# A hybrid attention, HGRN2 and mixture-of-experts block: two-operand work moved from GpSimd to VectorE, token-major mixer outputs, and an affine step moved behind a gather

## The chip, the core and the metric

The kernel runs on one core of one Trainium2 chip. The metric is device time in microseconds, the median of three runs. One execution was also taken by the hardware profiler; all rows below are from it. Engines: TensorE (PE, with its weight loads PEld), VectorE (DVE), ScalarE (ACT), GpSimd (POOL) and SyncE (SP), which issues most transfers.

## What is computed

One encoder block on 256 tokens of width 1024, with 16 learned meta tokens in front (272 rows, all float32):

```
h    = layer_norm(concat(meta, x), ln_emb)
qa, ka, va, qb, fb, ib, gb = split(h @ w_in)              # 1024 x 3584
ya   = diff_attention(qa, ka, va)    # 4 heads, rope, chunk-causal, a = p0 - lam * p1, rms_norm per head
yb   = hgrn2(qb, fb, ib, gb)         # 4 heads, gated linear recurrence, rms_norm per head, * silu(g)
h    = layer_norm(alpha * h + concat(ya, yb) @ w_out, ln1)
ffn  = moe(h)                        # 32 experts, top 4 of each token, clamped SwiGLU
h    = layer_norm(alpha * h + ffn, ln2);  return h without the meta tokens
```

## The kernel before

The program has a first part (to about 204 us) that does everything up to the router, and a second part, the experts.

*Pieces.* w_in comes in 28 pieces of 128 output features (512 KB each), w_out in 8. `split(i)` takes a raw piece and makes two parts of it whose sum is the float32 weight: hi, a cast on ScalarE (L178), and lo = raw - hi (L180). The engine of the lo part is GpSimd for i < 3 and for odd i, 20 of 36 pieces, and VectorE for the rest. There are three slots for hi and lo each and four for raw pieces. `project i` runs 24 matmuls, for each of 8 blocks of k the products hi*hH, hi*hL and lo*hH, where hH and hL are the hi and lo parts of the normalised tokens, which VectorE makes block by block at the start (L241, L242). Its result goes on through a `post`, a function by kind of piece.

*The order.* TensorE's instructions stand in the order of the table STEPS, one line for a piece and what follows it; the other engines' order is made by the scheduler. The steps: `diagonal` and `level 0` to `level 7` are the HGRN2 recurrence as a doubling scheme (products of decays, L414, L416 and L418, the matmuls L408), `rope_q`, `rope_k` the rotations, `scores`, `turn` and `values_a` the attention, `out_a` and `out_b` the heads' outputs (features by tokens), `norm r` (the function `fin`) their rms norm with a column sum on TensorE (L496), a root on ScalarE (L498) and a reciprocal of 128x256 on VectorE (L499), `mix a n` the product with a piece of w_out. `residual` multiplies h by the first layer norm's gain and adds its bias on GpSimd (L291, L292), `fold` prepares the router. `begin`, `prefetch` and `close` release space or start the loads of expert weights.

*Behind the last mix.* total1, turn1, logits, choose and position make the second layer norm, the router's choice and each token's place in its expert. `affine(a)` normalises h and applies gain and bias (for half of the tokens' columns on VectorE, L676 and L677, the rest on ScalarE and GpSimd, L678 to L680). `gather` picks the tokens of the experts by a matmul with a 0/1 matrix G (L715) and copies the result to XT (L719).

*Experts.* Experts are served in units of 1 to 4 by the number of their tokens, each with six chunks of 2 MB that are streamed into ten buffers. L779 is the gate and up product, L793 the down product, `begin_acc` (L897, L898) starts the sum over experts with alpha * h and the down biases.

## Time and profile before

| | us |
|---|---|
| runs | 1130.12, 1131.45, 1132.07; median 1131.45 |
| profiled execution | 1132.66 (span 1130.8) |
| TensorE busy | 1007.2 (89%) |
| VectorE busy | 337.3 (30%) |
| ScalarE busy | 177.2 (16%) |
| GpSimd busy | 99.2 (9%) |
| moved by DMA | 428.44 MB, mean 379 GB/s |
| first matmul of the first expert (L779) | at 204.43 |

A busy share is an average over parts with different limits. In the page's forty slices the DMA engines are busy for 3 to 8 tenths up to the eighth slice and for 9 or more from the ninth (from 226 us on) to the thirty-ninth; GpSimd works in the first seven slices alone, apart from the last. A timeline row is: start, duration, engine, line, operation, out<-in and shape, how often, and in brackets how long the engine had been idle and which instruction ended that. A granted clock (PEclk) of 1.00 is 2.4 GHz, 0.50 is 1.2 GHz.

### The profile page before, as it was taken

What the parts mean: (1) busy time and instruction counts of PE and PEld (TensorE: products, weight loads), DVE (VectorE), ACT (ScalarE), POOL (GpSimd) and SP (SyncE); (2) the same over time, 40 slices, a digit from 0 to 9 for tenths busy, and PEclk for the clock granted to TensorE, in tenths of its full rate; (3) what the DMA queues carried; (4) which work ended last, traced back from release to release, by engine and by line L of the source; (5) the groups of instructions that cost most, each with busy time, mean ns of one, the idle gap of its engine ahead of it and who ended that gap; (6) DMA issues with size and microseconds to landing.
All of it is one profiled execution on the core that took longest, in us unless ns stands there. A gap on an engine that the chain in (4) does not pass through costs nothing.

```text
span 1130.8 us, 14815 instructions
## 1 busy us (share of the span) xinstructions
PE 1007.2 (89%) x6066; PEld 525.7 (46%) x6067; DVE 337.3 (30%) x721; ACT 177.2 (16%) x394; POOL 99.2 (9%) x91
## 2 busy tenths in 40 slices
...
GB/s 216 268 216 109 160 223 304 340 416 400 426 428 427 427 429 427 427 427 427 428 427 426 428 429 427 427 428 428 428 426 427 428 428 429 424 429 427 428 409 129
DMA packets 37022, 428.44 MB, mean 379 GB/s; under 512 B 4388, under 2 KB 4772, under 8 KB 12758
## 3 DMA queue, kind: packets, MB, share of 16 engines
...
q10 hardware_dynamic: 628, 0.74, 0.2%
...
## 4 chain that ended last, share of the span: by engine, by line
PE 71%; DMA 14%; DVE 6%; ACT 1%; issue 1%; POOL 0%; DVEq 0%; ACTq 0%; POOLq 0%
PE ps_pj L779 21%; DMA wchunk<-in_wexp 14%; PE ps_pj L793 10%; PE ps_s L715 5%; PE ps_pj L864 5%; PE ps_pj L319 4%; PE ps_s L828 4%; PE ps_pj L836 4%; PE ps_pj L828 4%; PE ps_s L897 3%; PE ps_pj L876 2%; PE ps_g L752 1%; PE ps_pj L774 1%; PE ps_s L408 1%; DVE acc L898 1%
## 5 line engine op out<-in xcount | busy, mean ns | idle before, releaser
L779 PE MATMUL ps_pj<-wchunk,XT 128*64 128x512 f32 x1088 | 245.2, 597 | 0.0
L742 DVE TENSOR_SCALAR g<-ps_pj 128x256 f32<-128x256 f32 x52 | 22.1, 425 | 512.5 <-PE ps_pj L779 243.6
L864 PE MATMUL ps_pj<-wchunk,XT 128*32 128x512 f32 x768 | 113.4, 685 | 39.2 <-DMA wchunk<-in_wexp 39.2
L779 PEld LDWEIGHTS ps_pj<-wchunk,XT 128*64 128x64 f32 x1088 | 73.4, 137 | 137.9 <-issue 137.6
L793 PE MATMUL ps_pj<-wchunk,at 128*64 128x256 f32 x1088 | 123.7, 382 | 1.6 <-DVE at L754 1.6
L743 ACT ACTIVATE sgm<-g 128x256 f32<-128x256 f32 x58 | 24.2, 416 | 497.8 <-DVE g L742 497.8
L793 PEld LDWEIGHTS ps_pj<-wchunk,at 128*64 128x64 f32 x1088 | 75.8, 137 | 43.0 <-issue 3.2
L319 PE MATMUL ps_pj<-c,whi 128*128 128x272 f32 (+1 forms) x420 | 84.8, 296 | 0.7 <-DVE c L241 0.4
L762 POOL CAST sel<-sels 128x128 fp32r<-128x128 f32 (+2 forms) x30 | 10.5, 349 | 841.9 <-PE ps_g L752 248.9
L864 PEld LDWEIGHTS ps_pj<-wchunk,XT 128*32 128x32 f32 x768 | 27.5, 122 | 118.0 <-issue 64.0
L715 PE MATMUL ps_s<-G,h 128*128 128x128 f32 (+1 forms) x480 | 61.7, 290 | 15.2 <-DVE G L697 13.9
L876 PE MATMUL ps_pj<-wchunk,at 128*32 128x256 f32 x768 | 58.1, 447 | 17.2 <-DMA wchunk<-in_wexp 8.3
L715 PEld LDWEIGHTS ps_s<-G,h 128*128 128x128 f32 x480 | 58.7, 203 | 27.2 <-DVE G L697 24.4
L319 PEld LDWEIGHTS ps_pj<-c,whi 128*128 128x128 f32 x420 | 68.2, 194 | 2.4 <-DVE c L241 0.8
L319 PE MATMUL ps_pj<-c,wlo 128*128 128x272 f32 (+1 forms) x224 | 64.7, 289 | 0.0
L180 POOL TENSOR_TENSOR wlo<-wraw,whi 128x1024 fp32r<-128x1024 f32 x20 | 51.4, 2573 | 60.6 <-ACT whi L178 60.6
L876 PEld LDWEIGHTS ps_pj<-wchunk,at 128*32 128x32 f32 x768 | 28.8, 127 | 43.2 <-issue 19.6
L897 PE MATMUL ps_s<-Y,C 128*128 128x512 f32 (+1 forms) x104 | 47.8, 602 | 0.0
L178 ACT CAST whi<-wraw 128x1024 fp32r<-128x1024 f32 x36 | 37.6, 1047 | 59.0 <-PE ps_pj L319 28.4
L799 ACT COPY Y<-ps_pj 64x256 f32<-64x256 f32 x68 | 24.9, 366 | 137.8 <-PE ps_pj L793 137.4
L319 PEld LDWEIGHTS ps_pj<-c,wlo 128*128 128x128 f32 x224 | 43.2, 193 | 0.0
L836 PE MATMUL ps_pj<-wchunk,at 128*128 128x512 f32 x96 | 42.2, 592 | 0.0
...
## 6 DMA issues: line engine op xcount, KB each, us to landing
wchunk<-in_wexp SPq DMA_DIRECT2D x189, 2048.0 KB, 28.1
...
```

The lines of the kernel that those rows point to most:

```text
L178: nc.scalar.copy(hi, raw)
L180: eng.tensor_tensor(lo, raw, hi.bitcast(F32), op=OP.subtract)
L319: nc.tensor.matmul(b[:, 0:n], w[:, ks], v[:, L - n:L], start=(k == 0 and j == 0), stop=(k == KT - 1 and j == 2))
L715: nc.tensor.matmul(bs[k // 4][:, k % 4 * P:k % 4 * P + ns], h[:, a, k * P:(k + 1) * P], G[:, a].rearrange("p n w -> p (n w)"), start=(a == ...
L779: nc.tensor.matmul(gu[ab * 64:(ab + 1) * 64, :], X[:, kh * 4 + k, u * SL:(u + 1) * SL], wv[:, k, ab * 512:(ab + 1) * 512], start=False, st ...
L793: nc.tensor.matmul(dn[c][ab * 64:(ab + 1) * 64, 0:256], aTs[f // 4][:, f % 2, f // 2 % 2 * 64:f // 2 % 2 * 64 + 64], wv[:, f, ab * 256:(ab ...
L799: nc.scalar.copy(Y[u * 64:(u + 1) * 64, c * 512 + ab * 256:c * 512 + (ab + 1) * 256], dn[c][ab * 64:(ab + 1) * 64, 0:256])
L828: nc.tensor.matmul(gus[ab], X[:, kh * 4 + k, :], wv[:, k, ab * 512:(ab + 1) * 512], start=False, stop=(kh == 1 and k == 3))
L836: nc.tensor.matmul(dn[c], aT[f // 2][:, f % 2, :], wv[:, f, :], start=(f == 0), stop=(f == KT - 1))
L864: nc.tensor.matmul(gu[q * 32:(q + 1) * 32, :], X[:, kh * 4 + k, us], wv[q // 2][:, k, q % 2 * 512:(q % 2 + 1) * 512], start=False, stop=(k ...
L876: nc.tensor.matmul(dn[q * 32:(q + 1) * 32, 0:256], at[:, f % 2, f // 2 * 32:(f // 2 + 1) * 32], wv[q // 2][:, f, q % 2 * 256:(q % 2 + 1) * ...
L897: nc.tensor.matmul(o, C[:, a, :], Y[0:C.shape[0], cs], start=True, stop=True)
```

## The change

1. *VectorE takes GpSimd's two-operand work:* all 36 lo parts, the residual's four products and sums (now behind `meta`, and their two loads in the ring of raw pieces), Tn in `hg_level`, the rope's cosine product, the lo part of bgu. GpSimd keeps the meta tokens' small products and some casts.
2. *Two first pieces together:* `both 0` interleaves pieces 0 and 1 block by block. `keep_busy` puts matmuls of the identity with itself, whose results nobody reads, ahead of and between the first transposes and between the two halves of the first gather. The second token tile is normalised half on VectorE and half on ScalarE.
3. *Token-major mixer outputs:* `out_a` and `out_b` give tokens by features, so a norm is a sum along the row (ScalarE's accumulator, L519), a root and a reciprocal of 128x2, a product (yt) and two transposes, with the gains applied behind them.
4. *Steps moved:* norms later, `turn 0 0` behind piece 24.
5. *LN affine behind the gather:* h stays normalised without gain and bias; XT gets them at evacuation, as a column each; the expert sum gets the gain by a matmul with a row of ones and the bias as a 33rd row of bdn.
6. *Router fold:* one matmul over 256 columns and a reduction in place of eight.

The core of the diff:

```diff
 STEPS = """
-project 0
-project 1, split 3, prefetch 1, split 4
+both 0
+split 3, prefetch 1, split 4
...
-project 9, lam, split 11, values_b 0, residual, split 12, level 0
+project 9, lam, split 11, values_b 0, split 12, level 0
...
-project 17, meta, split 19
+project 17, meta, residual, split 19
...
-project 19, split 21, rope_q 0, out_b 0, rope_q 1, norm 4, out_b 2, split 22
-project 20, split 23, norm 5, rope_k 1, out_b 3
-project 21, rope_q 2, norm 6, scores 0 0, norm 7
-project 22, rope_k 2, prefetch 1
-project 23, scores 0 1, split 24, split 25, turn 0 0, scores 1 0
-project 24, rope_k 3, scores 1 1, turn 0 1, split 26, split 27
+project 19, split 21, rope_q 0, out_b 0, rope_q 1, out_b 2, split 22
+project 20, split 23, norm 5, norm 4, rope_k 1, out_b 3
+project 21, rope_q 2, norm 6, scores 0 0
+project 22, norm 7, rope_k 2, prefetch 1
+project 23, scores 0 1, split 24, split 25, scores 1 0
+project 24, turn 0 0, rope_k 3, scores 1 1, turn 0 1, split 26, split 27
...
-mix 1 1, prefetch 3, norm 2, mix 1 2, out_a 3, mix 1 3, norm 3, split 32, mix 0 3, split 33, split 34, mix 1 4
+mix 1 1, prefetch 3, norm 2, mix 1 2, out_a 3, mix 1 3, split 32, mix 0 3, norm 3, split 33, split 34, mix 1 4
@@ split
-        eng = nc.gpsimd if i < 3 or i % 2 else nc.vector
-        eng.tensor_tensor(lo, raw, hi.bitcast(F32), op=OP.subtract)
+        nc.vector.tensor_tensor(lo, raw, hi.bitcast(F32), op=OP.subtract)
@@ row_bcast
-        t = t4(name)
+        t = pool.tile([P, D], F32, name=name, tag="raw", bufs=RAW)
@@ the first layer norm
+    def keep_busy(dst, n):
+        for _ in range(n):
+            nc.tensor.matmul(dst, ident, ident, start=True, stop=True)
+    keep_busy(tb[7][:, 384:512], 9)
...
-        nc.vector.tensor_scalar(src, src, mu, rs, op0=OP.subtract, op1=OP.mult)
+        if c0 > NM:
+            nmr = small.tile([P, 1], F32, name="nmr")
+            nc.vector.scalar_tensor_tensor(nmr, mu, -1.0, rs, op0=OP.mult, op1=OP.mult)
+            nc.vector.tensor_scalar(src[:, 0:512], src[:, 0:512], mu, rs, op0=OP.subtract, op1=OP.mult)
+            nc.scalar.activation(src[:, 512:1024], src[:, 512:1024], AF.Identity, bias=nmr, scale=rs)
+        else:
+            nc.vector.tensor_scalar(src, src, mu, rs, op0=OP.subtract, op1=OP.mult)
...
+        keep_busy(tb[7][:, 384:512], more)
@@ router_fold
-        for k in range(KT):
-            nc.tensor.matmul(b[:, NE:2 * NE], ones, wr[:, k, :], start=(k == 0), stop=(k == KT - 1))
+        nc.tensor.matmul(b[:, P:P + KT * NE], ones, wr.rearrange("p k e -> p (k e)"), start=True, stop=True)
@@ residual
-            nc.gpsimd.tensor_tensor(h[:, a, :], h[:, a, :], eg, op=OP.mult)
-            nc.gpsimd.tensor_tensor(h[:, a, :], h[:, a, :], eb, op=OP.add)
+            nc.vector.tensor_tensor(h[:, a, :], h[:, a, :], eg, op=OP.mult)
+            nc.vector.tensor_tensor(h[:, a, :], h[:, a, :], eb, op=OP.add)
@@ new
+    def both(i):
+        bs = []
+        for q in range(2):
+            bs.append((bank("g" if q else "pj"), parts.pop(i + q)) + posts[i + q])
+        for k in range(KT):
+            ks = slice(k * P, (k + 1) * P)
+            for b, (whi, wlo), n, _ in bs:
+                for j, (w, v) in enumerate(((whi, hH[:, k]), (whi, hL[k]), (wlo, hH[:, k]))):
+                    nc.tensor.matmul(b[:, 0:n], w[:, ks], v[:, L - n:L], start=(k == 0 and j == 0),
+                                     stop=(k == KT - 1 and j == 2))
+        for b, _, n, post in bs:
+            post(b[:, 0:n])
@@ square, fin
+        ss = small.tile([P, 2], F32, name="ss", bufs=3)
+        for a in range(2):
+            sq = t1("sq")
+            nc.scalar.activation(sq[:, 0:P], o[:, a, :], AF.Square, accum_out=ss[:, a:a + 1])
...
-        nc.tensor.matmul(c[:, 0:T], ones, sq[:, 0:T], start=True, stop=True)
-        sd = t1("sdr")[:, 0:T]
-        nc.scalar.activation(sd, c[:, 0:T], AF.Sqrt, bias=epst, scale=1.0 / P)
-        nc.vector.reciprocal(sd, sd)
+        nc.scalar.activation(ss, ss, AF.Sqrt, bias=epst, scale=1.0 / P)
+        nc.vector.reciprocal(ss, ss)
+        yt = t1("yt")[:, 0:T].rearrange("p (a v) -> p a v", a=2)
+        nc.vector.tensor_tensor(yt, o, ss[:, :, None].to_broadcast([P, 2, P]), op=OP.mult)
+        c = bank("g")[:, 0:T]
+        for a in range(2):
+            nc.tensor.transpose(c[:, a * P:(a + 1) * P], yt[:, a, :], ident)
@@ out_b
-        nc.tensor.matmul(o, vbm[:, hs], ATm[:, hh, :], start=True, stop=False)
-        nc.tensor.matmul(o[:, 0:P], vb[:, 0, hs], ATd[:, hh, 0, :], start=False, stop=False)
-        nc.tensor.matmul(o[:, P:T], vb[:, 0, hs], ATx[:, hh, :], start=False, stop=False)
-        nc.tensor.matmul(o[:, P:T], vb[:, 1, hs], ATd[:, hh, 1, :], start=False, stop=True)
+        token_major(4 + hh, [[(ATm[:, hh, 0:P], vbm[:, hs]), (ATd[:, hh, 0, :], vb[:, 0, hs])],
+                             [(ATm[:, hh, P:T], vbm[:, hs]), (ATx[:, hh, :], vb[:, 0, hs]),
+                              (ATd[:, hh, 1, :], vb[:, 1, hs])]])
@@ affine, now normal
-            nc.vector.scalar_tensor_tensor(ha[:, 0:c0], ha[:, 0:c0], mu, g1[:, 0:c0], op0=OP.subtract, op1=OP.mult)
-            nc.vector.scalar_tensor_tensor(ha[:, 0:c0], ha[:, 0:c0], rs, b1[:, 0:c0], op0=OP.mult, op1=OP.add)
-        nc.scalar.activation(ha[:, c0:], ha[:, c0:], AF.Identity, bias=nmr, scale=rs)
-        nc.gpsimd.tensor_tensor(ha[:, c0:], ha[:, c0:], g1[:, c0:], op=OP.mult)
-        nc.gpsimd.tensor_tensor(ha[:, c0:], ha[:, c0:], b1[:, c0:], op=OP.add)
+        nc.scalar.activation(h[:, a, :], h[:, a, :], AF.Identity, bias=nmr, scale=rs)
@@ gather
+                keep_busy(lg[:, 0, 4:8, :].rearrange("p q e -> p (q e)"), 5)
...
+            if k >= 4:
+                nc.vector.tensor_scalar(XT[:, k, 0:ns], src, gk, bk, op0=OP.mult, op1=OP.add)
+            else:
+                nc.scalar.activation(XT[:, k, 0:ns], src, AF.Identity, bias=bk, scale=gk)
@@ begin_acc
+        for c in range(2):
+            cs = slice(c * 512, (c + 1) * 512)
+            g1 = bank("s")
+            nc.tensor.matmul(g1, ones[0:1, :], acc[0:1, 0, cs], start=True, stop=True)
+            for a in (1, 0):
+                nc.vector.scalar_tensor_tensor(acc[:, a, cs], h[:, a, cs], ALPHA, g1, op0=OP.mult, op1=OP.mult)
```

Three places show how the order of the instructions moves. VectorE at the start, from the normalisation of the second token tile to the first casts (h is the tokens, c_76 their hi and lo parts, st and rs the statistics); before:

```order
L234 TENSOR_SCALAR h<-h,mv_e,rs_e 128x1024
L222 RECIPROCAL rs_e<-sd_e 128x1
L234 TENSOR_SCALAR h<-h,mv_e,rs_e 128x1024
L241 CAST c_76<-h_184 128x272
L242 TENSOR_TENSOR c_76<-h_184,c_76 128x272
```

and with the change:

```order
L245 TENSOR_SCALAR h<-h,mv_e,rs_e 128x1024
L179 TENSOR_TENSOR wlo<-wraw,whi 128x1024
L220 RECIPROCAL rs_e<-sd_e 128x1
L241 SCALAR_TENSOR_TENSOR nmr<-mv_e,rs_e 128x1
L242 TENSOR_SCALAR h<-h,mv_e,rs_e 128x512
L179 TENSOR_TENSOR wlo<-wraw,whi 128x1024
L253 CAST c_76<-h_207 128x272
L253 CAST c_76<-h_211 128x272
L254 TENSOR_TENSOR c_76<-h_207,c_76 128x272
```

Two lo pieces now stand between the normalisations on VectorE, one ahead of the second tile's reciprocal and one behind its first half.

ScalarE around the last attention head (c_78 with ps_s is the softmax's Exp, sdr or ss the norm's root, yHL the hi part of a head's output); before:

```order
L525 ACTIVATE c_78,z<-ps_s,mx 128x272 x2
L498 ACT_TABLE_LOAD
L498 ACTIVATE sdr<-ps_g,epst 128x256
L490 ACTIVATE sq<-ps_s 128x256
L498 ACTIVATE sdr<-ps_g,epst 128x256
L506 CAST yHL<-y_1725 128x256
L543 COPY c_78<-ps_g 16x128
L544 COPY c_78<-ps_g 128x256
```

and with the change:

```order
L557 ACT_TABLE_LOAD
L557 ACTIVATE c_78,z<-ps_s,mx 128x272 x2
L576 COPY c_78<-ps_g 128x256
L537 ACTIVATE yHL<-ps_g,sub_242 128x256
L519 ACTIVATE sq,ss<-ps_s 128x128 x2
L524 ACT_TABLE_LOAD
L524 ACTIVATE ss<-ss,epst 128x2
L537 ACTIVATE yHL<-ps_g,sub_242 128x256
```

Before, one table load stands behind the last Exp, and the roots follow it; now one load stands ahead of that Exp and one behind it.

VectorE behind the last mixers (st, mv, rs the second layer norm's statistics, lgs the logits, m, i and f the choice, eq and msk the mask that the first position waits for); before:

```order
L218 BN_AGGR mv_l_1958<-st_l_1955 128x2
L649 MAX m_1907<-lgs 128x8
L676 SCALAR_TENSOR_TENSOR h<-h,mv_l_1958,g_649 128x512
L222 RECIPROCAL rs_l_1962<-sd_l_1960 128x1
L650 MAX_INDEX i_1978<-m_1907,lgs 128x8
L684 TENSOR_SCALAR nm<-m_1907 128x1
L673 SCALAR_TENSOR_TENSOR nmr<-mv_l_1958,rs_l_1962 128x1
L652 CAST f_1981<-i_1978 128x8
L677 SCALAR_TENSOR_TENSOR h<-h,rs_l_1962,b_651 128x512
L654 TENSOR_TENSOR eq<-con,f_1981 128x128
L656 TENSOR_REDUCE msk<-eq 128x32
```

and with the change:

```order
L216 BN_AGGR mv_l_2012<-st_l_2009 128x2
L683 MAX m_1961<-lgs 128x8
L684 MAX_INDEX i_2032<-m_1961,lgs 128x8
L710 TENSOR_SCALAR nm<-m_1961 128x1
L220 RECIPROCAL rs_l_2016<-sd_l_2014 128x1
L686 CAST f_2035<-i_2032 128x8
L705 SCALAR_TENSOR_TENSOR nmr<-mv_l_2012,rs_l_2016 128x1
L688 TENSOR_TENSOR eq<-con,f_2035 128x128
L690 TENSOR_REDUCE msk<-eq 128x32
```

The two products with g and b between the choice and eq are gone.

## Rows read from the trace of the kernel before

**Rows 1.** The page, part 4: shares of the chain that ended last.
```profile
PE 71%; DMA 14%; DVE 6%; ACT 1%; issue 1%; POOL 0%; DVEq 0%; ACTq 0%; POOLq 0%
```

**Rows 2.** Windows of core 0: busy us of each engine, clock, DMA share, GB/s.
```profile
core 0: us, PE busy (x) PEld busy (x) DVE busy (x) ACT busy (x) POOL busy (x), PEclk, DMA share, GB/s
0.00:204.50 204.50, 180.01 (x1245) 159.57 (x1248) 150.64 (x282) 91.09 (x185) 85.92 (x59) 0.97 0.60 220
194.40:204.50 10.10, 8.79 (x61) 8.09 (x63) 4.91 (x21) 2.42 (x8) 2.58 (x4) 0.66 0.96 402
204.00:208.00 4.00, 4.00 (x19) 1.24 (x18) 1.60 (x13) 0.00 (x0) 0.00 (x0) 1.00 0.07 19
262.00:1106.00 844.00, 760.16 (x4408) 335.15 (x4402) 162.75 (x376) 71.48 (x177) 9.42 (x27) 0.96 1.01 427
```

**Rows 3.** Timeline of VectorE, 8 to 20 us: start us, us, instruction [idle before].
```profile
8.64 0.76 DVE L234 TENSOR_SCALAR h<-h,mv_e,rs_e 128x1024 f32<-128x1024 f32 x1
...
10.29 2.55 DVE L234 TENSOR_SCALAR h<-h,mv_e,rs_e 128x1024 f32<-128x1024 f32 x1
14.03 1.20 DVE L241 CAST c<-h 128x272 fp32r<-128x272 f32 x1 [1.18 <-ACT h L239]
...
19.33 2.49 DVE L242 TENSOR_TENSOR hL<-h,c 128x272 fp32r<-128x272 f32 x1
```

**Rows 4.** Timeline of GpSimd, 8 to 67 us.
```profile
9.95 5.12 POOL L180 TENSOR_TENSOR wlo<-wraw,whi 128x1024 fp32r<-128x1024 f32 x2 [9.47 <-ACT whi L178]
...
53.13 5.92 POOL L291 TENSOR_TENSOR h<-h,eg 128x1024 f32<-128x1024 f32 x2
59.01 2.80 POOL L180 TENSOR_TENSOR wlo<-wraw,whi 128x1024 fp32r<-128x1024 f32 x1
61.77 5.20 POOL L292 TENSOR_TENSOR h<-h,eb 128x1024 f32<-128x1024 f32 x2
```

**Rows 5.** Timeline of TensorE, 15 to 195 us: the places of the sum.
```profile
15.28 1.07 PE L319 MATMUL ps_pj<-c,whi 128*128 128x272 f32 x2 [0.41 <-DVE c L241]
...
25.53 0.52 PE L319 MATMUL ps_pj<-c,whi 128*128 128x272 f32 x2 [0.32 <-ACT sgn L359]
...
35.69 1.97 PE L282 MATMUL ps_g<-wr,con 128*128 128x32 f32 x16
...
62.48 2.75 PE L408 MATMUL ps_s<-c 128*128 128x64 f32 x16 [2.66 <-DVE c L416]
...
70.38 2.00 PE L408 MATMUL ps_s<-c 128*128 128x64 f32 x16 [0.95 <-DVE c L416]
...
75.11 1.90 PE L408 MATMUL ps_s<-c 128*128 128x64 f32 x16
...
133.32 0.28 PE L540 MATMUL ps_g<-con,c 128*16 128x128 f32 x1 [2.96 <-DVE c L530]
...
142.84 0.28 PE L540 MATMUL ps_g<-con,c 128*16 128x128 f32 x1 [0.89 <-DVE c L530]
...
194.40 0.41 PE L662 MATMUL ps_g<-msk,con 128*128 128x32 f32 x2 [2.17 <-DVE msk L656]
```

**Rows 6.** Groups by line on VectorE, 0 to 204.5 us: xcount | busy us, mean ns | idle.
```profile
L180 DVE TENSOR_TENSOR wlo<-wraw,whi 128x1024 fp32r<-128x1024 f32 x16 | 21.2, 1325 | 7.4 <-ACT whi L178 7.3
L499 DVE RECIPROCAL sdr<-sdr 128x256 f32<-128x256 f32 x8 | 14.0, 1749 | 0.8 <-ACT sdr L498 0.7
L414 DVE TENSOR_TENSOR c<-c 128x512 f32<-128x512 f32 x5 | 10.0, 1996 | 8.1 <-issue 4.2 <-PE ps_s L412 2.2 <-POOL h L292 1.7
...
L414 DVE TENSOR_TENSOR c<-c,Tn 128x512 f32<-128x512 f32 x3 | 2.0, 675 | 0.0
```

**Rows 7.** Timeline of TensorE: out_b of the second HGRN2 head, 103.9 us.
```profile
103.93 0.69 PE L560 MATMUL ps_s<-c,vm 16*128 16x256 f32 x2
104.56 0.49 PE L561 MATMUL ps_s<-c 128*128 128x128 f32 x2
104.88 0.39 PE L562 MATMUL ps_s<-c,c 128*128 128x128 f32 x2
105.11 0.39 PE L563 MATMUL ps_s<-c 128*128 128x128 f32 x2
```

**Rows 8.** Timeline of ScalarE, 161 us: the table load before the last norms.
```profile
161.37 1.28 ACT L498 ACT_TABLE_LOAD   x1
```

**Rows 9.** Timeline of VectorE behind the last mixer, 189 to 193 us.
```profile
189.43 1.33 DVE L676 SCALAR_TENSOR_TENSOR h<-h,mv_l,g 128x512 f32<-128x512 f32 x1
...
190.97 2.02 DVE L673 SCALAR_TENSOR_TENSOR nmr<-mv_l,rs_l 128x1 f32<-128x1 f32 x1
...
192.99 0.74 DVE L677 SCALAR_TENSOR_TENSOR h<-h,rs_l,b 128x512 f32<-128x512 f32 x1
```

More of the change, by code (lines that the diff above doesn't have):

```diff
@@ L202, in build @@
     bgu = cpool.tile([P, 2, 512], F32R, name="bgu")
-    rows = {}
     nc.sync.dma_start(con[:, P:], consts_d[:, P:])
@@ L544, in a_turn, with token_major @@
         nc.scalar.copy(aT0[:, a * P:(2 * a + 1) * P], c[:, P:(a + 2) * P])
+    def token_major(row, terms):
+        o = bank("s")[:, 0:T].rearrange("p (a v) -> p a v", a=2)
+        for a in range(2):
+            for j, (w, v) in enumerate(terms[a]):
+                nc.tensor.matmul(o[:, a, :], w, v, start=(j == 0), stop=(j == len(terms[a]) - 1))
+        square(row, o)
     def out_a(hh):
@@ L597, in close @@
         rings.append(ctx.enter_context(tc.tile_pool(name="ring2", bufs=1)))
-    do = dict(project=lambda i: project(i, *posts[i]), split=split, prefetch=prefetch, fold=router_fold, residual=residual,
+    do = dict(both=both, project=lambda i: project(i, *posts[i]), split=split, prefetch=prefetch, fold=router_fold, residual=residual,
               diagonal=hg_diag, lam=lam, level=hg_level, meta=hg_meta, out_a=out_a, out_b=out_b, norm=fin, scores=scores,
@@ L665, in position, with normal @@
         nc.vector.scalar_tensor_tensor(psm[:, a, :], cn[:, a, :], 1.0, msk[:, a, :], op0=OP.add, op1=OP.mult)
[L667 to L669 removed]
+    def normal(a):
         mu, rs = mus[a]
[L671 removed]
         nmr = small.tile([P, 1], F32, name="nmr")
         nc.vector.scalar_tensor_tensor(nmr, mu, -1.0, rs, op0=OP.mult, op1=OP.mult)
[L674 to L680 removed]
+        nc.scalar.activation(h[:, a, :], h[:, a, :], AF.Identity, bias=nmr, scale=rs)
     def weigh(a):
@@ L717, in gather @@
                                  stop=(a == 1 and k % 4 == 3))
-        for c in range(2):
-            (nc.vector.tensor_copy if c else nc.scalar.copy)(XT[:, c * 4:(c + 1) * 4, 0:ns],
-                                                             bs[c].rearrange("p (k s) -> p k s", s=P)[:, :, 0:ns])
+        for k in range(KT):
+            src, gk, bk = bs[k // 4][:, k % 4 * P:k % 4 * P + ns], vec[:, V_G1 + k:V_G1 + k + 1], vec[:, V_B1 + k:V_B1 + k + 1]
+            if k >= 4:
+                nc.vector.tensor_scalar(XT[:, k, 0:ns], src, gk, bk, op0=OP.mult, op1=OP.add)
+            else:
+                nc.scalar.activation(XT[:, k, 0:ns], src, AF.Identity, bias=bk, scale=gk)
         return XT
@@ L944, in gates_turn @@
     def gates_turn():
-        late["bdn"] = t4("bdn", (NE, D))
-        nc.scalar.dma_start(late["bdn"], bdn_d)
-        late["gT"] = gT = t1("gT", (NE, T))
+        late["bdn"] = bdn = t4("bdn", (NE + 1, D))
+        nc.scalar.dma_start(bdn[0:NE], bdn_d)
+        nc.scalar.dma_start(bdn[NE:NE + 1], rows_d[3:4])
+        late["gT"] = gT = t1("gT", (NE + 1, T))
+        nc.vector.memset(gT[NE:NE + 1], ALPHA)
         for a in range(2):
```

69 lines of the change are left out of this document (30 added, 39 removed).

## The prediction

> **What bounds the kernel now.** I read four views, from the end of the program towards its start. First, the shares of the chain that ended last [rows 1]: TensorE holds 71% of it and the weight stream 14%, so the kernel looks bound by TensorE. The windows [rows 2] say where. From 262 us to 1106 us the DMA engines are busy all the time (share 1.01, 427 GB/s), while TensorE has 84 us of idle time in those 844: there the expert weights set the pace. Nothing in the change makes them fewer bytes. Just before, at 204 to 208 us, the DMA share is 0.07: all buffers are full and the stream stands still until the first expert frees one. So the first expert's start (204.5 us) sets when the stream goes on, and a microsecond saved before it should come out at the end as a microsecond. The question is what happens to the first 204.5 us.
>
> In them TensorE is busy for 180.0 of 204.5 us and VectorE for 150.6 [rows 2]. Third view: TensorE's own rows [rows 5] with what ended each wait. VectorE ends them all: 2.66 us at 62.48, 0.95 at 70.38, 2.96 at 133.32, 0.89 at 142.84, 2.17 at 194.40. Fourth: why VectorE is late. The same TENSOR_SCALAR of 128x1024 takes 0.76 us at 8.64 and 2.55 us at 10.29 [rows 3]; beside the second lie two lo pieces on GpSimd, from 9.95 on [rows 4]. The level product L414 averages 0.675 us in the form with Tn and 1.996 us in the other [rows 6], whose instances at 56 to 67 us lie beside GpSimd's h*eg, lo piece and h+eb [rows 4]. VectorE seems to stand still until GpSimd's two-operand instruction has finished. Taking the difference of long and short instances over all such groups (the first is L414 with 5 x 1.32 = 6.6 us, the last the two rows at 10.29 and 19.33), some 36 us of VectorE's 150.6 are waiting of this kind.
>
> **The change, part by part.** The sum is against the profiled execution, 1132.66 us (span 1130.8); the median of the runs is 1.2 us less.
>
> *Start.* Before, the first piece's matmuls begin at 15.28 and the third piece at 25.53 [rows 5]. On VectorE the 2.55 us at 10.29 become one lo piece, about 1.2 (L180's mean of 1.325 contains long ones), and half of 0.76: 0.9 less. The first cast, 1.20 at 14.03 [rows 3], falls to about 0.3: 0.9 less. So the matmuls begin near 13.5. A level and a piece take 4.73 us (70.38 to 75.11) and the level 1.90 of it [rows 5], so a piece's 24 matmuls take about 2.85. Two interleaved pieces are 5.7, with 0.4 for catching up with the last hL, which takes 2.49 us at 19.33 now and should take under 0.5: the third piece starts near 19.6. That is **-5.9**, with bounds of -4 (the clock stays low for the first 3.7 us, as the double pitch of matmuls after 15.28 shows it now, and the fillers don't change it) and -6.6 (no catching up).
>
> *Router fold.* Sixteen matmuls of 1.97 us at 35.69 [rows 5] become one pair over 256 columns, about 0.45: **-1.5**. VectorE's added reduction lies beside the next piece.
>
> *Levels 0 and 1.* The waits of 2.66 and 0.95 us go if L414 and L416 return to 0.68. Behind the first wait the clock is at its lower level (level 0 takes 2.75 us against 1.90 at 75.11): from 62.48 to the end of work at 69.43 pass 6.95 us, against 4.73 for a level and a piece and 0.2 for the values' three matmuls, 2.05 more. Together **-5.65**; bounds -3 (half the stretch stays) and -5.65. VectorE takes the lo pieces and the four residual products (about 1.2 each, as L180); the residual is now behind level 7, and its rows are covered by pieces 17 and 18 unless the eg and eb loads, now in the ring of raw pieces, come late.
>
> *95 to 155 us.* Waits of 2.96 and 0.89 go, since turn 0 0 stands one piece later and L529 no longer waits for GpSimd: -3.85. In place of them come waits in the norms: the new path is two squares, a root, a reciprocal of 128x2, a product and two transposes, and its transposes stand on TensorE only one piece behind. I put +2.3 on norm 4 and norm 6, where the gap is shortest; bounds 0 and 4. Net **-1.55**.
>
> *Token-major outputs.* Old out_b: 0.63 us for the two rows of L560 with 16-row weights, 0.32 for L561, then 0.23 each [rows 7], 1.4 in all. A 128-column step is 0.23 alone, and each change between 16 and 128 rows of weights adds 0.1 to 0.2. Five such matmuls with three or four changes: about 1.7. Eight heads at +0.3 are +2.4; the transposes in the norm replace a 256-column product for half its time, -0.2 each, -1.6. Net **+0.8**, nearest to L560's own rows; the lower bound is five steps without any change's cost, 5 x 0.23 = 1.15, which makes -3.6, and the upper one four changes of 0.2 each, +4. By the Trainium skill ("TensorE: Matmul & The Clock Gate", The mechanism) a weight load is pulled ahead of matmuls in flight when it goes to a row group that doesn't conflict or to the background buffer, which would make the changes free and the sum 4.4 lower; the steps with 16-row weights don't show that here.
>
> *Last mixers, 155 to 182 us.* ScalarE now alternates between Sqrt and Exp for the norms and the scores. Its order holds four more table loads than before; one takes 1.28 us [rows 8]. VectorE loses the reciprocals of 1.749 us [rows 6], four of which lie in this stretch, and gets four lo pieces of 1.2. I let half of the table loads show: **+2.2**, bounds -1 and +5.1.
>
> *Behind the last mix.* VectorE's L676 takes 1.33 us at 189.43 and nmr 2.02 at 190.97, and L677 0.74 at 192.99 [rows 9]; the change drops L676 and L677, and nmr should be 0.16. All three stand one behind the other ahead of msk, so the change is 3.9 us earlier at the wait of 194.40. In the stretch 194.4 to 204.5 the granted clock is 0.66 [rows 2], which the five fillers may lift: 8.79 us of work would be 5.8 at full clock; I count 0.8 of these 3. Against it: the fillers themselves, a full-width ScalarE normalisation, eight evacuations of 128 columns in place of two, +1.6. Net **-3.1**, bounds -1.5 and -5.
>
> *Experts.* begin_acc gets two matmuls and four more VectorE steps, the gathers eight small evacuations each. They lie where DMA sets the pace; the share of 1.01 has no hole to fill. **+0.5** for the first gathers; bounds 0 and 1.5.
>
> Sum: -5.9 - 1.5 - 5.65 - 1.55 + 0.8 + 2.2 - 3.1 + 0.5 = **-14.2**: 1118.5 us in a profiled execution, **1117.2 us** against the median.
>
> **The rivals.** *A, fewer new waits.* The norms' waits (2.3) don't show, the table loads are hidden by the mixes (2.2), and the transitions of weights cost nothing (about 1): gain 19.7, 1111.8 us. For it: between 142.84 and 194.40 TensorE hardly waits now [rows 5], so mixers stand ready to cover a late norm. Against it: the order puts an Exp between two roots at the very end.
>
> *B, ScalarE takes VectorE's place.* All four table loads stand on the path (5.1 in place of 2.2), the norm waits are 4, and the start keeps its low clock (4 in place of 5.9): gain 14.2 - 2.9 - 1.7 - 1.9 = 7.7, 1123.7 us. The point where it decides is the first Sqrt behind the last scores: the norm of the last attention head can't start before it. The Trainium skill ("ScalarE: Activation LUTs", Rules for kernel authors) says to group functions by table set and to budget about 2.7 us for each switch. With that figure four switches would be 10.8 us and this rival 1129.4; the trace has 1.28 for one [rows 8], and it decides.
>
> *C, slower.* VectorE becomes the bound of the first part. If GpSimd is not the reason for the long instances, they stay long, and VectorE gets about 39 us of added work (20 lo pieces at 1.2 = 24, eight cosine products at about 0.4, with fewer columns than L414's 512 at 0.675, residual 4.8, eight yt products, smaller ones) and loses about 19 (eight reciprocals by 1.6, affine, sdr*sg, y). That is +20 us on an engine busy 150.6 of 204.5 us; if its idle 54 us are all dependency waits, the first expert starts 20 us later less the fold's 1.5: 1150 us. It decides from the point where less than 20 of the 36 us of stretching go away. Against it: where no GpSimd instruction is near, the same forms are short.
>
> *D, the front's gain is not handed on.* If the weight chunks before the first expert can't be fetched earlier, the stream ends at most as much earlier as its own holes before 262 us allow, about 5 us (4 x 0.93 at 204 to 208, and the rest behind it): 1126 us. Against it: the buffers of those chunks come free with the mixers, which move forward too.
>
> **How the numbers follow.** Forecast 0.47, A 0.22, B 0.20, C 0.04, D 0.07. The predicted time is the forecast's, 1117.2. The range takes A with some of its unsized gains (the token-major term at its lower end, -4.4 more: 1107.5) and B up to 1125; C, most of D, and the tails of the others are left out, about 2 in 10. Differences of 0.2% (2.3 us) are what a measurement of this kernel can tell from no change. Faster: all of forecast, A and B, and most of D: 0.94. Within 0.2%: 0.02, the far end of D. Slower: C, 0.04.
>
> **What would show it.** In the changed profile, VectorE's instructions of one form should have one length (L414's successor 0.68 in every instance). The third piece should start near 19.6 us. The waits before levels 0 and 1 should be gone, and the clock there full. Between 155 us and the last mix I look for ScalarE table loads of 1.28 and for TensorE's waits on yHL; the first expert's matmuls should start near 190, and the DMA share of 0.07 before its first freed buffer should be there for a shorter time. A long VectorE instruction with no GpSimd instruction beside it, or a first expert that starts early with an end that doesn't move, would make the prediction wrong.

## The result, and the profile after

| | before | changed |
|---|---|---|
| median, us | 1131.76 (1130.12 to 1134.12, 4 runs) | 1120.97 (1117.79 to 1121.93, 4 runs) |
| profiled execution, us | 1132.66 | 1120.72 (span 1118.9) |
| first matmul of the first expert, us | 204.43 | 189.13 |

The ratio is 0.9891, interval 0.9868 to 0.9914: faster by 10.8 us at the medians, 11.9 in the profiled executions, where 14.2 was forecast. The time lies in the range. Two later measurements of the same kernel gave 1119.03 and 1120.16.

The page's totals and shares of the chain that ended last, to set beside [rows 1]:

```profile
PE 1012.7 (91%) x6130; PEld 532.0 (48%) x6131; DVE 331.9 (30%) x811; ACT 198.7 (18%) x468; POOL 17.5 (2%) x47
...
PE 79%; DMA 13%; DVE 5%; issue 1%; ACT 1%; SPq 0%; DVEq 0%
```

GpSimd has gone from 99.2 to 17.5 us, the chain's DMA share is nearly the same. The windows, which answer to [rows 2]:

```profile
core 0: us, PE busy (x) PEld busy (x) DVE busy (x) ACT busy (x) POOL busy (x), PEclk, DMA share, GB/s
0.00:189.10 189.10, 180.01 (x1303) 162.28 (x1304) 132.79 (x323) 99.57 (x217) 4.15 (x15) 0.98 0.64 224
...
189.00:193.00 4.00, 4.00 (x23) 1.28 (x24) 1.98 (x14) 0.00 (x0) 0.00 (x0) 1.00 1.02 377
262.00:1094.00 832.00, 750.60 (x4356) 333.72 (x4356) 166.44 (x407) 83.13 (x215) 9.48 (x27) 0.95 1.00 425
600.00:605.00 5.00, 5.00 (x31) 3.08 (x32) 1.63 (x6) 0.19 (x1) 0.00 (x0) 0.64 1.02 433
740.00:755.00 15.00, 15.00 (x52) 5.90 (x52) 1.12 (x2) 0.59 (x1) 0.00 (x0) 1.00 0.92 366
```

The first expert starts 15.3 us earlier, more than the forecast wanted (14.7). VectorE's work ahead of it has fallen from 150.6 to 132.8 us, though it took over the two-operand work: the stretching is gone. At 189 to 193 us the stream now runs (1.02, before 0.07 at the same place). The last two rows belong to the loss behind it: a low clock at 600 to 605, and a stream at 0.92 at 740 to 755.

VectorE's timeline at the start (answers to [rows 3]), and its groups by line (answer to [rows 6]):

```profile
13.86 0.30 DVE L253 CAST c<-h 128x272 fp32r<-128x272 f32 x1 [0.94 <-ACT h L251]
...
18.27 0.43 DVE L254 TENSOR_TENSOR hL<-h,c 128x272 fp32r<-128x272 f32 x1
```

```profile
L440 DVE TENSOR_TENSOR c<-c 128x512 f32<-128x512 f32 x5 | 3.4, 688 | 1.8 <-PE ps_s L438 1.8
...
L525 DVE RECIPROCAL ss<-ss 128x2 f32<-128x2 f32 x8 | 1.3, 164 | 5.8 <-ACT ss L524 5.7
```

Nearly every form has one length now; the levels' predicated copies take 1.32 and 1.31, then 0.71 to 0.73 us, nearly as before and with no GpSimd instruction beside them. The 2.49 us of the last hL are 0.43, L440 (L414 before) has 0.688 where it had 1.996, and a norm's reciprocal, of 128x2 now, 0.164 where it had 1.749.

TensorE's timeline at the places of the sum (answers to [rows 5] and, at 138 us, to [rows 7]):

```profile
14.62 0.80 PE L344 MATMUL ps_pj<-c,whi 128*128 128x272 f32 x2
...
20.86 0.41 PE L331 MATMUL ps_pj<-c,whi 128*128 128x272 f32 x2
...
30.89 0.70 PE L293 MATMUL ps_g<-wr,con 128*128 128x256 f32 x2
...
53.44 1.89 PE L434 MATMUL ps_s<-c 128*128 128x64 f32 x16
...
105.09 0.44 PE L530 MATMUL ps_g<-con,yt 128*128 128x128 f32 x2 [0.91 <-DVE yt L527]
...
112.50 0.44 PE L530 MATMUL ps_g<-con,yt 128*128 128x128 f32 x2 [1.18 <-DVE yt L527]
...
138.01 0.48 PE L583 MATMUL ps_s<-vm,c 16*128 16x128 f32 x2
138.42 0.49 PE L583 MATMUL ps_s<-c 128*128 128x128 f32 x2
...
139.89 0.52 PE L547 MATMUL ps_s<-c 64*128 64x144 f32 x4
...
146.10 0.31 PE L572 MATMUL ps_g<-con,c 128*16 128x128 f32 x1 [0.80 <-DVE ps_s L551]
...
150.22 0.28 PE L488 MATMUL ps_g<-con,c 128*16 128x128 f32 x1 [0.22 <-ACT c L576]
...
181.83 2.05 PE L742 MATMUL ps_s<-G,h 128*128 128x128 f32 x16 [0.62 <-DVE G L729]
183.71 1.28 PE L234 MATMUL ps_g<-con 128*128 128x128 f32 x10
...
189.13 3.65 PE L809 MATMUL ps_pj<-wchunk,XT 128*64 128x512 f32 x16
```

The levels' waits are gone: the matmuls that [rows 5] has at 62.48, behind a wait of 2.66 and 2.75 us long, start at 53.44 without one and take 1.89. (They are those of level 1, and the next wait, 0.95, was that of level 2; the prediction counts them as levels 0 and 1.) New are the norms' waits (0.91, 1.18), an out_a of 1.88 us from 138.01 to 139.89, the wait of 0.80 at 146.10, and the gather's fillers (1.28 at 183.71). ScalarE's table loads in the last mixers, where one stood before [rows 8]:

```profile
140.65 1.28 ACT L524 ACT_TABLE_LOAD   x1
...
142.40 1.28 ACT L557 ACT_TABLE_LOAD   x1
...
145.23 1.28 ACT L524 ACT_TABLE_LOAD   x1
...
147.56 1.28 ACT L557 ACT_TABLE_LOAD   x1
...
153.29 1.28 ACT L524 ACT_TABLE_LOAD   x1
```

### The profile page after: what moved, and what is told of

It reads as the page before. It is cut to its first block, busy times and chain, and to the rows that moved or that the text cites. A ratio compares the mean times of both kernels' runs of the same rounds, so it can differ in the third digit from the quotient of the medians.

```text
span 1118.9 us, 15037 instructions
## 1 busy us (share of the span) xinstructions
PE 1012.7 (91%) x6130; PEld 532.0 (48%) x6131; DVE 331.9 (30%) x811; ACT 198.7 (18%) x468; POOL 17.5 (2%) x47
## 4 chain that ended last, share of the span: by engine, by line
PE 79%; DMA 13%; DVE 5%; issue 1%; ACT 1%; SPq 0%; DVEq 0%
PE ps_pj L809 22%; DMA wchunk<-in_wexp 13%; PE ps_pj L823 11%; PE ps_pj L331 7%; PE ps_s L742 5%; PE ps_pj L894 5%; PE ps_s L858 4%; PE ps_pj L866 4%; PE ps_pj L858 4%; PE ps_s L927 3%; PE ps_pj L906 2%; PE ps_s L583 1%; PE ps_g L782 1%; PE ps_pj L804 1%; PE ps_s L434 1%
## 5 line engine op out<-in xcount | busy, mean ns | idle before, releaser
L331 PE MATMUL ps_pj<-c,whi 128*128 128x272 f32 (+1 forms) x390 | 76.4, 290 | 0.0
L331 PEld LDWEIGHTS ps_pj<-c,whi 128*128 128x128 f32 x390 | 61.5, 188 | 1.0 <-ACT c L474 0.4
L331 PE MATMUL ps_pj<-c,wlo 128*128 128x272 f32 (+1 forms) x208 | 59.3, 285 | 0.0
L179 DVE TENSOR_TENSOR wlo<-wraw,whi 128x1024 fp32r<-128x1024 f32 x36 | 44.0, 1221 | 18.3 <-ACT whi L178 18.2
L858 PE MATMUL ps_pj<-wchunk,XT 128*128 128x512 f32 x96 | 41.7, 592 | 0.0
L858 PE MATMUL ps_s<-wchunk,XT 128*128 128x512 f32 x96 | 41.7, 592 | 0.0
```

Source lines behind the costliest of these rows:

```text
L179: nc.vector.tensor_tensor(lo, raw, hi.bitcast(F32), op=OP.subtract)
L331: nc.tensor.matmul(b[:, 0:n], w[:, ks], v[:, L - n:L], start=(k == 0 and j == 0), stop=(k == KT - 1 and j == 2))
L858: nc.tensor.matmul(gus[ab], X[:, kh * 4 + k, :], wv[:, k, ab * 512:(ab + 1) * 512], start=False, stop=(kh == 1 and k == 3))
```

## The experiments

All times are medians; "first expert" is the start of its first matmul in the profile. Before was measured beside each group: 1133.2 (runs 1 to 4), 1131.92 (5 to 8), 1131.56 (9 to 12); runs of different groups are best compared by their ratios.

| run | median, us | ratio to before (interval) | first expert, us |
|---|---|---|---|
| 1 changed, again | 1119.03 | 0.9881 (0.9846 to 0.9916) | 189.24 |
| 2 lo pieces on GpSimd | 1128.04 | 0.9958 (0.9938 to 0.9979) | 197.43 |
| 3 before, lo pieces on VectorE | 1127.91 | 0.9949 (0.9928 to 0.9970) | 200.91 |
| 4 old outputs and norms | 1122.39 | 0.9904 (0.9870 to 0.9939) | 194.35 |
| 5 late roots | 1119.05 | 0.9878 (0.9846 to 0.9910) | 189.15 |
| 6 no fillers | 1118.46 | 0.9879 (0.9842 to 0.9916) | 188.04 |
| 7 no gain in the sum | 1121.08 | 0.9898 (0.9861 to 0.9934) | 189.56 |
| 8 before, residual moved | 1131.87 | 0.9994 (0.9977 to 1.0011) | 204.24 |
| 9 pieces 0 and 1 apart | 1120.84 | 0.9897 (0.9876 to 0.9918) | 193.71 |
| 10 later roots, no fillers in the gather | 1115.45 | 0.9849 (0.9830 to 0.9867) | 185.94 |
| 11 as 10, one-hots early | 1115.02 | 0.9843 (0.9822 to 0.9864) | 185.91 |
| 12 changed, third time | 1120.16 | 0.9898 (0.9878 to 0.9918) | 189.25 |

**Run 1, the changed kernel again.** No edit.

> The changed kernel, unaltered, once more. Its profile lost 3.2 us of TensorE's lead between 594 and 612 us, where the granted clock was at its lower level during one gather, and the expert part as a whole gave back 3.4 of the 15.3 us that the first expert had gained. Theory 1 (chance): the low clock at that gather is not tied to the kernel; this profile has it at another gather or nowhere, the first expert starts at 189.1 again within 0.5 us, and the total is 1117 to 1122. Theory 2 (the expert part of the change itself, its longer start of the sum over experts): the same 3 us are lost in this profile too, at the same places.

Windows of run 1, at the last mixers and at the gather that had the low clock:

```profile
152.00:156.00 4.00, 4.00 (x16) 3.15 (x16) 1.07 (x3) 2.52 (x6) 0.00 (x0) 0.68 0.96 414
...
600.00:605.00 5.00, 5.00 (x48) 3.05 (x45) 0.41 (x1) 0.73 (x2) 0.00 (x0) 1.00 1.00 426
```

At 600 to 605 the clock is 1.00, in the first profile 0.64. TensorE's lead at the products behind it is 13.7 us here and 9.8 there; the span is 1116.9 against 1118.9. Theory 1 holds for that gather. But 1.4 us of lead are lost here too, between the gathers at 232 and 370 us.

**Run 2, the lo pieces back.**

```diff
-        nc.vector.tensor_tensor(lo, raw, hi.bitcast(F32), op=OP.subtract)
+        eng = nc.gpsimd if i < 3 or i % 2 else nc.vector
+        eng.tensor_tensor(lo, raw, hi.bitcast(F32), op=OP.subtract)
```

> The changed kernel with the 20 lo pieces back on GpSimd, nothing else. Theory 1 (VectorE stands still until a two-operand instruction of GpSimd has ended): VectorE loses 24 us of work and still becomes later; two-operand instructions of VectorE show lengths above 2 us again, the first expert starts 4 to 8 us later (193 to 197), total 1124 to 1129. Rival (the long instances of before had another cause, so VectorE's work is what counts): VectorE is freer, the first expert starts at 186 to 189, total at most 1121.

VectorE's timeline of run 2 at the start:

```profile
10.46 2.02 DVE L242 SCALAR_TENSOR_TENSOR nmr<-mv_e,rs_e 128x1 f32<-128x1 f32 x1
...
14.77 2.08 DVE L254 CAST c<-h 128x272 fp32r<-128x272 f32 x1 [1.84 <-ACT h L252]
...
20.95 2.50 DVE L255 TENSOR_TENSOR hL<-h,c 128x272 fp32r<-128x272 f32 x1
```

A step on one column takes 2.02 us and a cast 2.08, and although VectorE has 24 us less to do, the first expert is 8.2 us later than in run 1 and the median 9.0. Theory 1; the first expert is even 0.4 us beyond its range. Against run 1, 5.1 us are lost before the third piece, 2 more by the sixth, and 0.4 at the levels: level 1 starts without a wait, though lo pieces stand on GpSimd beside the levels (at 50.40 and 60.44):

```profile
59.25 1.89 PE L435 MATMUL ps_s<-c 128*128 128x64 f32 x16
```

**Runs 3 and 8, one half each on the kernel before.** Run 3 puts the lo pieces on VectorE; run 8 moves the residual alone:

```diff
-project 9, lam, split 11, values_b 0, residual, split 12, level 0
+project 9, lam, split 11, values_b 0, split 12, level 0
-project 17, meta, split 19
+project 17, meta, residual, split 19
-            nc.gpsimd.tensor_tensor(h[:, a, :], h[:, a, :], eg, op=OP.mult)
-            nc.gpsimd.tensor_tensor(h[:, a, :], h[:, a, :], eb, op=OP.add)
+            nc.vector.tensor_tensor(h[:, a, :], h[:, a, :], eg, op=OP.mult)
+            nc.vector.tensor_tensor(h[:, a, :], h[:, a, :], eb, op=OP.add)
```

> The kernel before with all 36 lo pieces on VectorE, nothing else. Theory 1: the long instances beside lo pieces go, those beside the residual's and the rope's products on GpSimd stay; the first expert starts 4 to 9 us earlier (195 to 200), total 1122 to 1128. Rival (VectorE becomes the bound, with 24 us more work): the first expert starts at 205 to 215, total 1132 to 1142.

> The kernel before with the residual's four products and sums on VectorE behind the meta step, nothing else. Theory 1 (the waits at levels 0 and 1 come from GpSimd's h*eg and h+eb, not from its lo pieces): the waits of 2.66 and 0.95 us and the low clock at level 0 go, the first expert starts 4.5 to 6 us earlier (198.5 to 200), total 1126 to 1129. Rival (the lo pieces beside the levels are enough for the waits): less than 2.5 us at the first expert, total 1130 to 1133.

TensorE around the levels, in run 3 (a wait at the diagonal, L388, and one at level 1) and then in run 8 (levels 0 and 1):

```profile
51.30 0.71 PE L388 MATMUL ps_s<-c 128*128 128x128 f32 x4 [2.66 <-DVE c L370]
...
62.18 2.10 PE L407 MATMUL ps_s<-c 128*128 128x64 f32 x16 [1.60 <-DVE c L415]
```

```profile
57.59 3.68 PE L408 MATMUL ps_s<-c 128*128 128x64 f32 x16 [2.65 <-DVE c L394]
...
65.31 1.89 PE L408 MATMUL ps_s<-c 128*128 128x64 f32 x16
```

VectorE and GpSimd of run 8 ahead of its wait:

```profile
50.31 2.76 DVE L291 TENSOR_TENSOR h<-h,eg 128x1024 f32<-128x1024 f32 x2
...
54.10 2.35 POOL L180 TENSOR_TENSOR wlo<-wraw,whi 128x1024 fp32r<-128x1024 f32 x1
...
54.20 3.34 DVE L394 TENSOR_TENSOR c<-c 128x1024 f32<-128x1024 f32 x1
```

Run 3 gains 3.5 us at the first expert, a little below the 4 to 9 that theory 1 gave, and 5.3 in the median, inside its range; the rival had said that it would be slower. With the residual still on GpSimd, waits of 2.66 us at the diagonal and 1.60 at level 1 are left.

Run 8 gains 0.2 us at the first expert and nothing in the median. These are the rival's numbers, but not for its reason: the waits ahead of levels 1 and 2 are gone, as theory 1 said, with the lo pieces still on GpSimd. What took the gain is a new wait of 2.65 us at level 0, with the clock at 0.50 behind it (3.68 us for what took 1.90 before). Its rows name the cause. The load of the residual's gains was issued at 43.2 us, so they had landed and VectorE took the two products at 50.31, ahead of L394, which took 1.22 before and now took 3.34 beside a lo piece. In the changed kernel the load is issued at 85.1 and the products stand at 88.83, behind the levels.

Runs 2, 3 and 8 together say that GpSimd's residual made the levels' waits. In run 2 the lead over the kernel before grows from 0.4 to 6.2 us there: the levels' 5.75 us come out with the lo pieces left on GpSimd. No run moves the residual alone to a late place.

**Run 4, the old outputs and norms** (`square`, `fin`, `out_a`, `out_b` as before, in the changed order).

> The changed kernel with the old mixer outputs and norms (features by tokens, column sum on TensorE, reciprocal of 128x256 on VectorE), in the changed order of steps. Theory 1 (token-major outputs cost TensorE and ScalarE more than they save on VectorE): one table load instead of five in the last mixers, outputs 0.4 us shorter per head; the first expert starts 2 to 4 us earlier (185 to 187), total 1115 to 1119. Rival (the reciprocals of 1.75 us on VectorE are the larger cost): waits of 1 to 2 us before the norms' products, the first expert at 189 to 193, total 1119 to 1124.

TensorE's timeline of run 4 around the first norms:

```profile
105.36 0.73 PE L506 MATMUL ps_g<-c,mixc 128*128 128x272 f32 x2 [2.21 <-ACT sdr L524]
...
113.81 0.70 PE L522 MATMUL ps_g<-sq,con 128*128 128x256 f32 x2 [1.26 <-DVE rt L508]
...
124.68 1.21 PE L541 MATMUL ps_s<-c 64*128 64x144 f32 x4 [0.78 <-ACT c L551]
```

The rival is right that it gets slower: the first expert is 5.2 us later than in the first profile, beyond the rival's 189 to 193, and the median is 3.4 us above run 1's and inside the rival's range, though the two intervals overlap. That the reciprocals are the cause is shown only in part. 8.8 us are lost by the first product with w_out (149.57 against 140.81). From 105 to 125 us VectorE is busy for 17.2 of 20 us and ends two of TensorE's four waits (1.26, and 0.67 at 123.21). ScalarE ends the other two (2.21 and 0.78), each behind a table load, and the clock is 0.50 at 125 to 130 us. Then 3.5 us come back: the last mixers have one table load and shorter outputs. Rival C's mechanism is at work here, but not alone.

**Run 5, late roots.** The root's bias is made from the last Exp's sum, so that ScalarE can't take it earlier; norm 0 and norm 1 also stand a step later in the table:

```diff
+        if (hh, a) == (3, 1):
+            late_eps["t"] = small.tile([P, 1], F32, name="epl", bufs=1)
+            nc.vector.tensor_scalar(late_eps["t"], z[:, 1:2], 0.0, EPS, op0=OP.mult, op1=OP.add)
...
-        nc.scalar.activation(ss, ss, AF.Sqrt, bias=epst, scale=1.0 / P)
+        nc.scalar.activation(ss, ss, AF.Sqrt, bias=late_eps.get("t", epst), scale=1.0 / P)
```

> The changed kernel with the four attention heads' roots tied to the last Exp (their bias is made from its sum), and norm 0 and norm 1 each one step later: one table load in the last mixers in place of five. Theory 1 (of the 4.8 us that the token-major form loses in this stretch, the table loads and the low clock behind their wait are most): the waits of 0.8 and 0.2 at 146 and 150 us and the low clock there go, the first expert starts 2 to 3.5 us earlier (185.5 to 187.2), total 1115 to 1118. Rival (the outputs' change between 16 and 128 rows of weights is the cost, 0.4 us a head): the first expert within 1 us of 189.2, total 1118 to 1120.

```profile
150.21 0.41 PE L531 MATMUL ps_g<-con,yt 128*128 128x128 f32 x2 [1.28 <-DVE ss L526]
```

The line is TensorE's only wait in that stretch. Four table loads less, and no time gained: the norm now waits for the last Exp and the one load behind it, and a clock of 0.58 at 152 to 156 us follows the wait. The rival's number came, but not for its reason, as run 10 shows.

**Run 6, no fillers** (`keep_busy` returns at once).

> The changed kernel without the matmuls whose results nobody reads. Theory 1 (they lift the clock for the first pieces and for the gather): the first two pieces run at the lower clock for some 3 us, the third piece starts 1 to 2 us later than 20.9, the gather takes 2.7 to 3.8 us in place of 2.05 for a half; first expert 190.5 to 193, total 1120 to 1123. Rival (they stand in the way: ten of them at 10.66 us end only at 12.8, behind the second tile's first half): the second tile's transposes start 0.5 us earlier, the first expert at 188.5 to 189.5, total 1117.5 to 1119.5.

TensorE's timeline of run 6 at the first gather:

```profile
181.85 2.05 PE L741 MATMUL ps_s<-G,h 128*128 128x128 f32 x16 [0.63 <-DVE G L728]
...
184.98 2.02 PE L741 MATMUL ps_s<-G,h 128*128 128x128 f32 x16 [0.70 <-DVE G L728]
```

and of the kernel before at the same place:

```profile
195.50 2.71 PE L715 MATMUL ps_s<-G,h 128*128 128x128 f32 x16 [0.70 <-DVE G L703]
...
199.51 3.79 PE L715 MATMUL ps_s<-G,h 128*128 128x128 f32 x16 [0.61 <-DVE G L703]
```

Both halves take what they took with fillers, less than before, and the second starts 1.1 us earlier: there the fillers stood in the way, and something else in the change lifted the clock. At the start it depends on the profile. First to third piece takes 7.39 us without them (13.47 to 20.86) and 6.24 with them; the third piece comes as early as in the first profile (20.86) but 1.2 us later than in run 1 (19.70). The ten fillers between the two token tiles, in the first profile and in run 1:

```profile
10.66 2.34 PE L234 MATMUL ps_s<-con 128*128 128x128 f32 x10
```

```profile
9.97 1.28 PE L234 MATMUL ps_s<-con 128*128 128x128 f32 x10
```

In the first profile they took 1.06 us longer, and the second tile's transposes stood behind them without a wait for VectorE. So the fillers at the start won 1.2 us or nothing.

**Run 7, begin_acc without the gain.**

> The changed kernel without the gain of the second layer norm in the residual sum over experts: two matmuls, four steps on VectorE and one small load less in begin_acc; the gain of that norm is left out of the residual path. Theory 1 (the longer begin_acc costs the TensorE lead that the expert part gives back, 1.9 us and some waits): TensorE's lead at the products behind it is larger by 1.5 to 2.3 us, and as far as TensorE bounds the experts up to 800 us the total is 1116.5 to 1118. Rival (the weight stream bounds the experts; what begin_acc costs is hidden): the total is 1118 to 1120, within 0.5 us of the unaltered kernel.

The median, 1121.08, lies above both ranges, and its interval can't be told from the unaltered kernel's: the rival in the main. Behind begin_acc TensorE is 6.7 us earlier than in run 1 (264.20 against 270.86), more than theory 1 said, and at the next gather 1.8 us later (326.79 against 324.95). The longer begin_acc is hidden.

**Run 9, pieces 0 and 1 apart.**

> The changed kernel with pieces 0 and 1 one after the other instead of interleaved; all else as changed. Theory 1 (the interleaving is what hides the wait for the last hL block): piece 0 waits 1 to 1.5 us for the last hL blocks as they come one per 0.6 us while a block's three matmuls take 0.36, the third piece starts 1 to 1.5 us later against the first matmul (7.2 to 7.7 in place of 6.24), total 1119.5 to 1122. Rival (the normalisation's shorter instances did it all): less than 0.3 us.

First to third piece takes 7.83 us in place of 6.24, a little more than theory 1 has it: piece 0 takes 4.52 us (14.71 to 19.23), three of its rows 0.79 us where the others take 0.41; the first expert's further 2.9 us are a low clock in this profile's last mixers, and the median is 0.7 us above run 12's, which the intervals can't tell apart.

**Runs 10 to 12, a better version.** Run 10 is run 5 with norm 0 behind more work, and without the gather's fillers; run 11 also makes the one-hot matrices early; run 12 is the changed kernel beside them.

```diff
-turn 3 0, split 30, turn 2 1, mix 0 1, norm 0, values_a 3, out_a 2, mix 0 2, norm 1, turn 3 1, mix 1 0, split 31
+turn 3 0, split 30, turn 2 1, mix 0 1, values_a 3, mix 0 2, mix 1 0, turn 3 1, norm 0, out_a 2, norm 1, split 31
...
-                keep_busy(lg[:, 0, 4:8, :].rearrange("p q e -> p (q e)"), 5)
```

> The changed kernel with the roots tied to the last Exp and norm 0 and norm 1 behind the first product of the second token tile with w_out and turn 3 1, and without the five fillers between the halves of the first gather. Theory 1 (each wait in front of the last mixers costs its own length and the low clock behind it; the gather's fillers cost 1.1 us): no wait of more than 0.5 us and full clock between 140 and 160 us, the first expert 3 to 4 us earlier (185 to 186.5), total 1114.5 to 1117. Rival (the wait only moves to the next norm): the first expert at 187.5 to 188.5, total 1117 to 1120.

> As the run before, and in the experts VectorE makes each unit's one-hot matrix one chunk earlier than the gather that reads it. Theory 1 (TensorE's waits of 1.1 us before each gather, and the low clock that now and then follows one, take the lead of the first expert away): these waits go, no low clock between 400 and 800 us, the lead at the products of 600 us is at least that at the first expert less 1 us, total 1 to 3 us under the run before. Rival (from 262 us on the weight stream sets the pace, and the lead is only used up later): within 1 us of the run before.

> The changed kernel, unaltered, beside the two runs before this one, on the same chip: first expert at 189.1 within 0.3 us whatever the first matmul's time, since the lead of an early start is lost again in a wait and a low clock before the last mixers; total 1118 to 1122. If an early start is handed on instead, the first expert is at 188 where the first matmul is at 13.5.

TensorE's timeline of run 10, at the norms:

```profile
150.68 0.38 PE L531 MATMUL ps_g<-con,yt 128*128 128x128 f32 x2
...
153.50 0.41 PE L531 MATMUL ps_g<-con,yt 128*128 128x128 f32 x2 [0.55 <-ACT sq L520]
```

One wait of 0.55 is left, the clock stays at 1.00 from 140 to 164 us, and the first expert starts 3.3 us earlier than in run 12; the median is 4.7 us lower. Four table loads and the waits they made were worth some 2 us, once the norm had cover; the gather's fillers 1.1. Run 10's profile has the low clock at the same gather that the first profile had (5.51 us for what takes 3.78 in run 12):

```profile
591.26 5.51 PE L745 MATMUL ps_s<-G,h 128*128 128x64 f32 x32 [1.06 <-DVE G L727]
```

Run 11 has no such wait and no low clock from 400 to 800 us. Its TensorE reaches 600 us with 23 us of lead, and then this:

```profile
599.66 3.65 PE L812 MATMUL ps_pj<-wchunk,XT 128*64 128x512 f32 x16 [0.46 <-DMA wchunk<-in_wexp]
...
604.56 3.65 PE L812 MATMUL ps_pj<-wchunk,XT 128*64 128x512 f32 x16 [0.81 <-DMA wchunk<-in_wexp]
```

TensorE waits for the weight stream, chunk after chunk, and the median is 0.4 us below run 10's, which the intervals can't tell apart. The rival holds. Run 12 started its first piece 1.1 us before the first profile's, and its first expert is at 189.25 all the same. It lost the lead at 104 us, where a low clock follows a norm's wait (0.80 at 104 to 108 us, 0.78 at 108 to 112); run 1 lost it at the last mixers (0.68 at 152 to 156). That the three come out within 0.12 us is, as far as these runs show, a coincidence.

## Why the prediction was right, and where its sizes were off

Leads below are differences of the start of the same step in the two profiles, before against changed.

- *What bounds the kernel.* Held, and run 11 shows it from the other side: a lead of TensorE beyond the stream's buys nothing. The hole of 0.07 is used up now; run 10's further 3.3 us ahead of the first expert still came out in full.
- *Stretching by GpSimd.* Held (run 2). With the +20 us that rival C counts as added work, VectorE's fall from 150.6 to 132.8 us makes 38 us of stretching gone, an estimate, beside the 36 read from the rows. What I had not said is which work makes which wait: the lo pieces cost most of the start, the residual made the levels' waits (runs 2, 3 and 8), and moved work can make a new wait where it lands (run 8).
- *Start.* 4.7 us in the first profile (25.53 to 20.86), 5.8 in runs 1 and 12; forecast 5.9. The 1.1 between them are in the main the ten fillers' own time (run 6). The interleaving carries 1.6 of it.
- *Fold.* 1.45, forecast 1.5. *Levels.* The lead goes from 6.2 to 12.0: 5.75, forecast 5.65.
- *95 to 155 us, with out_b.* 2.1, forecast 1.15. The norms' waits, 0.91 and 1.18, are 2.1 of the 2.3 that I had put.
- *Outputs.* 1.88 us a head where the forecast had 1.7: a step with 16-row weights takes 0.41, one behind it 0.42, so each change costs about 0.2. By the prediction's own figures its upper bound is +2.8, not +4. The Trainium skill ("TensorE: Matmul & The Clock Gate", The mechanism) has a weight load pulled ahead of matmuls in flight when its row group doesn't conflict with theirs or when it goes to the background buffer. The prediction took that as a price at which these changes would be free; the rows at 138 us don't show them free.
- *Last mixers, with out_a.* The lead falls from 14.1 to 11.2, a loss of 2.9; forecast 2.6. The table loads did it as waits (0.80, 0.22) with a low clock behind them, clock 0.82 at 143 to 148. Rival B's mechanism was at work, at half its price.
- *Behind the last mix.* 4.1, forecast 3.1, and 5.3 without the fillers (run 6). Its parts came out otherwise. The 3.9 us on VectorE could give TensorE no more than its wait, 2.17 at 194.40. The full clock in the gather gave 2.4 (2.71 and 3.79 to 2.05 and 2.02) where 0.8 was counted, but not by the five fillers, which cost 1.1: the gather runs at full clock without them too. What lifted it stays open; the wait of 2.17 ahead of it is gone.
- *Experts.* This is the step that was mis-sized: **+0.5** was 3.4 in the first profile (15.3 at the first expert, 11.9 at the end), 1.3 in run 1 and 0.8 in run 12, by the spans. "They lie where DMA sets the pace" was right of begin_acc (run 7). What I had missed is that from 400 to 800 us TensorE has little slack, 390 of 400 us busy (391.5 before), and waits 1.1 to 1.2 us before each gather; in four of the fourteen profiles (the changed kernel's first, runs 3, 8 and 10) the clock falls at one such gather near 600 us, and 3 us of lead go. Then the stream stands for a moment (0.92 at 740 to 755, where run 1 has 1.00).

That the first expert came within 0.6 us of its forecast is in part luck: the start fell 1.2 short, and the stretch from 95 to 155 us and the one behind the last mix each gave about 1 more.

Without the 2.9 us by which the experts gave back more than forecast, the first profile would end at 1117.8, beside the 1118.5 forecast for it. Against the median of 1131.76 the forecast would be 1117.6, and 1120.97 came.
